# A decoder-layer step: the recurrence's levels two steps apart, the first transfers in another order, and half of the third chunk's post norm in that chunk's later stream

## The chip, the cores and the metric

The kernel runs on one core of one Trainium2 chip. Its time is the device time of one launch in microseconds (us). Each of the core's engines works through its own list of instructions in order: PE (TensorE) multiplies matrices, DVE (VectorE) and ACT (ScalarE) do the elementwise work, POOL (GpSimd) some of it, and SP (SyncE) mostly issues transfers between the chip's main memory and the core's on-chip memory. An instruction that waits holds up what stands behind it on its engine.

## The reference, cut to what matters

One layer of a decoder, in fp32, for 1,024 prompt tokens and for 8 running sequences with 8 new tokens each:

```
x = x + 1/2 * post1(swiglu_1(pre1(x)))                       # first feed-forward, D_FF = 2816
z = pre_mix(x) @ w_in + b_in                                  # q, k, v, f, i, gates in one projection
a = window attention, window 128, 8 heads, learned sinks      # sample: over cached keys and values
h = HGRN2 gated linear recurrence, 4 heads of 128 x 128       # sample: from a cached state
x = x + post_mix(concat(norm(a), gate(h)) @ w_out)
x = x + 1/2 * post2(swiglu_2(pre2(x)))                        # second feed-forward
```

The `pre` and `post` functions are RMS norms with a gain. The recurrence within a block of 128 tokens is computed by doubling: a level h = 1, 2, 4, ..., 64 joins neighbouring stretches of h tokens, multiplies queries and keys by the decays of those stretches, and yields the part of the attention-like matrix in which a query reads a key of the stretch before.

## The kernel before, in words

**Chunks.** The 1,088 tokens go in three chunks: chunk 0 has 320 columns (256 prompt tokens and the 64 of the samples) and is kept with features on the partitions; chunks 1 and 2 have 384 prompt tokens each. Every fp32 product is made of three products on split operands (`mm3`, lines 245, 246 and 247). The split is made on the core: a transfer brings a raw tile, ACT casts its high part (line 222), DVE subtracts to get the low part (line 223). Weights come into a ring of three raw tiles and leave as `wsph`/`wspl` (or `w`) tiles, of which there are eight.

**The feed-forward's second half** for chunks 1 and 2 is done by seven products of half-size operands. `pair(ms)` (from line 999 on) runs the products named in `ms` in turn: `PA` = (1, 6, 2) before the mixing, `PB` = (5, 3) behind chunk 0's input projection, then (7,) and (4,). For each group of two row blocks it needs a weight tile (line 951 or 954) and an activation tile `ar` (line 966), which is read back from main memory, cast by ACT and subtracted by DVE. Behind chunk 0's projection only one such `ar` tile is fetched ahead. The product's results are gathered from the PSUM banks by DVE (line 979) and, for product 5, by ACT as well (line 989); product 7 adds on POOL too (line 995). There are four `mm` banks; a group holds three.

**Side work.** What is not a feed-forward or projection product is written as generators that stop at each `yield`. `tick()`, called between groups of matmuls, advances them: named streams by a fixed rate, and two queues, `at` (attention) and `hg` (recurrence), at the pace at which the steps counted for a chunk end by its due tick (132, 208 and 256). The number beside a generator in a queue is the count of its steps. `intra(n)` (line 1250 on) is the recurrence inside the blocks of chunk n: for each level the matmuls `lv` (line 1267, up to h = 16) or `l` (line 1307, h = 32 and 64), the copies into `cm` (line 1297) or by ACT, and the multiplications of the queries by the decays on DVE (line 1316) and of the keys on POOL (line 1318). It stops once after each level.

**Post norm of chunks 1 and 2.** `half_n(y, hf, ...)` squares half of a chunk's columns on ACT (line 384), fetches a gain row (`gb`, line 377) and multiplies on DVE (line 388), three steps. `half1(n)` starts that for one half as the stream `half`, and `done1(n)` starts the stream `c1` or `c2` with the other half, then `post_n` (which reads x, writes `x1N` and normalises) and `pre_n` (the transposes `tr`, with ACT line 432 and DVE line 433 forming the projection's operand).

**The head.** `pre_first` forms chunk 0's first operands and issues, on SP, the loads of the first weight tiles (line 229) and of the rows of x (line 635), whose squares ACT sums (line 642) for the first norm. `wts.fill(k)` issues weight loads until k are ahead.

The written order is not the last word: within the dependences a scheduling pass settles each engine's list, so a moved step can move others.

Of the kernel before, what the change touches and what calls it, by code (L numbers as in the profile page):

```python
# [27 lines left out]
NPB = [2, 3, 3]  # L28
# [16 lines left out]
def tile_step(ctx: ExitStack, tc: tile.TileContext, A: dict, O: dict):  # L45
# [50 lines left out]
    def stream(name, gen, rate):  # L96
        streams[name] = [gen, rate, 0.0]
# [447 lines left out]
    def pre_first(wgu, h, wts):  # L545
# [83 lines left out]
        sm = small()  # L629
        V.memset(sm[:, 0], 1.0)  # L630
        rows = []
        for i in range(3):
            r = rows_of(0, i)
            t = big(F32, (P, D))
            nc.sync.dma_start(t[:r], A["x_prompt"][0, i * P:(i + 1) * P] if i < 2 else
                              A["x_sample"].rearrange("b t d -> (b t) d"))
            rows.append(t)

        def squares(i):
            r = rows_of(0, i)  # L640
            t = rows[i][:r]
            do("ACT", lambda: S.activation(t, t, AF.Square, scale=RMS, accum_out=sm[:r, 0, i:i + 1]))

        squares(0)
        squares(1)
        with queued("ACT"), queued("DVE"):
            wts.fill(2)
        last["ACT"], last["DVE"] = formed[1].ins, formed[0].ins
        squares(2)
        do("ACT", lambda: S.activation(junk[:, :P], ones, AF.Silu))  # L650
        do("DVE", lambda: V.tensor_scalar(ms0[:, 0:3], sm[:, 0, 0:3], EPS, None, op0=ALU.add))
        root(sm[:, 1, 0:3], ms0[:, 0:3])
# [390 lines left out]
    def mixing(tp, h):  # L1043
# [206 lines left out]
        def intra(n):  # L1250
# [40 lines left out]
            while h <= 64:  # L1291
# [37 lines left out]
                            G.tensor_copy(Av[:, j, :, r], C[r, j])  # L1329
                h *= 2  # L1330
                yield
            z["K"], z["D"] = K, Ds[0]

        def finish_hgrn(n, bank, r, c0):
# [182 lines left out]
        def ready(kind, n):  # L1517
            if n not in MT:
                MT[n] = new_h(n)
            if kind == "at":  # L1520
                gens = [(attn_block(n, b), 9) for b in range(NPB[n])]
                if n == 0:
                    gens += [(sample_attn(), 11), (kv_out(0), 1)]
                if n == 2:
                    gens.append((kv_out(2), 1))
            else:
                gens = [(intra(n), 8)] + [(hgrn_block(n, b), 3) for b in range(NPB[n])]
                if n == 0:
                    gens.append((sample_hgrn(), 14))
                if n == 2:  # L1530
                    gens.append((state_out(), 1))
            queues[kind] += [[n, g, left] for g, left in gens]
# [77 lines left out]
    def done1(n):  # L1610
        y, g = f1.ys[n], cols[:, C_MPRE:C_MPRE + 8]
        if n == 0:
            stream("c0", seq(post_t(y, A["x0T"], halfpost[:, 0:8], x1T, ms0), pre_t(y, g, hmix)), RA0)
        else:
            need("half")
            stream(f"c{n}", seq(half_n(y, 2 - n, sums[n], A["norm_ffn1_post"]),
                                post_n(n, y, sums[n], xN[n - 1], x1N[n - 1]), pre_n(n, y, g, hmix)), RA1)

    def half1(n):
# [38 lines left out]
    with tc.tile_pool(name="mx", bufs=1) as tp:  # L1658
        w_in_units, w_out_units = mixing(tp, hmix)
        need("c0")  # L1660
        now[0] = 0
        w_in_units(0)
        half1(1)
        f1.pair(PB, False, last=lambda: f1.begin_pair((7,), False))
        done1(1)
        f1.pair((7,), False, last=lambda: f1.begin_pair((4,), False))
        half1(2)
        f1.pair((4,), False)
        done1(2)
        need("c1")  # L1670
        w_in_units(1)
        need_mix(0)
        w_out_units(0, ym, sums)
        done_mix(0)
        need("c2")
        w_in_units(2)
        need("c0")
        f2.head(range(HEAD2[0]))
        need_mix(1)
        w_out_units(1, ym, sums)  # L1680
        done_mix(1)
        f2.head(range(HEAD2[0], HEAD2[1]))
        need("c1")
        need_mix(2)
        w_out_units(2, ym, sums)
        done_mix(2)
# [128 lines left out]
```

## Time and profile before

| | us |
|---|---|
| median of three runs | 1952.87 |
| the three runs | 1950.09, 1952.87, 1953.01 |
| the profiled execution | 1954.31 |
| its span (first to last instruction) | 1952.6 |
| PE busy in it | 1937.5 (99%) |
| DVE, ACT, POOL busy | 1349.6 (69%), 929.0 (48%), 211.1 (11%) |
| mean granted TensorE clock | 0.998 |

A row of a timeline gives start, busy time, engine, source line, operation, result and operands; in brackets stands the idle time of the engine before it and what ended it. The records of back-to-back matmuls overlap, so the time that one costs is read from one start to the next: 0.23 us for a 512-column one, 0.15 us for a 320-column one. The chain of waits follows the program's end back, piece by piece, to what released each piece.

### The profile page before, as it was taken

What the parts mean: (1) busy time and instruction counts of PE and PEld (TensorE: products, weight loads), DVE (VectorE), ACT (ScalarE), POOL (GpSimd) and SP (SyncE); (2) the same over time, 40 slices, a digit from 0 to 9 for tenths busy, and PEclk for the clock granted to TensorE, in tenths of its full rate; (3) what the DMA queues carried; (4) which work ended last, traced back from release to release, by engine and by line L of the source; (5) the groups of instructions that cost most, each with busy time, mean ns of one, the idle gap of its engine ahead of it and who ended that gap; (6) DMA issues with size and microseconds to landing.
All of it is one profiled execution on the core that took longest, in us unless ns stands there. A gap on an engine that the chain in (4) does not pass through costs nothing.

```text
span 1952.6 us, 34158 instructions
## 1 busy us (share of the span) xinstructions
PE 1937.5 (99%) x13451; PEld 1825.4 (93%) x13451; DVE 1349.6 (69%) x2188; ACT 929.0 (48%) x1637; POOL 211.1 (11%) x213
## 2 busy tenths in 40 slices
PE   9999999999999999999999999999999999999998
PEld 9999999999998987788899898999999999999887
DVE  5876667776558666875667765745987877655666
ACT  6633333444445544654345455745544444444453
POOL 0000000000004112111232431101000000000202
PEclk9999999999999999999999999999999999999999
DMA  9643345556677555675434333556555645577974
GB/s 322 209 143 129 144 162 186 179 183 208 236 236 228 163 146 163 213 228 153 120 101 141 115 112 117 190 166 206 174 204 187 217 177 186 206 237 232 308 260 141
DMA packets 162492, 362.65 MB, mean 186 GB/s; under 512 B 16524, under 2 KB 60236, under 8 KB 162316
## 3 DMA queue, kind: packets, MB, share of 16 engines
q1 hardware_dynamic: 161324, 358.65, 55.5%
q8 instruction: 105, 1.72, 0.4%
q10 hardware_dynamic: 1008, 1.84, 0.3%
q14 instruction: 55, 0.45, 0.1%
HBM read 283.78 MB, written 77.63 MB: 185 GB/s over the span
## 4 chain that ended last, share of the span: by engine, by line
PE 94%; DMA 2%; DVE 2%; ACT 1%; issue 1%; POOL 0%; SPq 0%; DVEq 0%; POOLq 0%; ACTq 0%
PE mm L245 28%; PE mm L247 28%; PE mm L246 28%; PE c L247 1%; PE c L245 1%; PE c L246 1%; DMA ar<-fa 1%; PE pv L1234 1%; PE sc L1193 1%; PE pT L1219 1%; PE lv L1267 0%; DMA raw<-in_ffn_w_gu_dram 0%; DMA x1N<-big 0%; PE av L1368 0%; DMA big<-in_x0T_dram 0%
## 5 line engine op out<-in xcount | busy, mean ns | idle before, releaser
L245 PE MATMUL mm<-h,wsph 128*128 128x320 f32 (+1 forms) x1280 | 409.5, 320 | 0.2 <-DVE sg L702 0.2
L247 PE MATMUL mm<-h,wspl 128*128 128x320 f32 (+1 forms) x1280 | 403.5, 317 | 1.2 <-DVE wspl L223 1.2
L246 PE MATMUL mm<-h,wsph 128*128 128x320 f32 (+1 forms) x1280 | 404.4, 316 | 0.0
L223 DVE TENSOR_TENSOR wspl<-raw,wsph 128x1024 fp32r<-128x1024 f32 x200 | 250.0, 1251 | 156.4 <-ACT wsph L222 156.0
L222 ACT CAST wsph<-raw 128x1024 fp32r<-128x1024 f32 x200 | 209.3, 1048 | 270.6 <-PE mm L246 205.4
L222 ACT CAST w<-raw 128x512 fp32r<-128x512 f32 (+1 forms) x226 | 169.3, 754 | 240.3 <-PE mm L246 119.8
L223 DVE TENSOR_TENSOR w<-raw,w 128x512 fp32r<-128x512 f32 (+1 forms) x226 | 196.6, 874 | 87.8 <-ACT w L222 87.3
L245 PEld LDWEIGHTS mm<-h,wsph 128*128 128x128 f32 x1280 | 240.4, 188 | 5.4 <-issue 3.2
L247 PEld LDWEIGHTS mm<-h,wspl 128*128 128x128 f32 x1280 | 239.9, 188 | 3.0 <-DVE wspl L223 1.7
L246 PEld LDWEIGHTS mm<-h,wsph 128*128 128x128 f32 x1280 | 240.5, 188 | 1.5 <-issue 0.7
L245 PE MATMUL mm<-h,w 128*128 128x384 f32 x704 | 235.6, 335 | 0.0
L246 PE MATMUL mm<-h,w 128*128 128x384 f32 x704 | 235.6, 335 | 0.0
L247 PE MATMUL mm<-h,w 128*128 128x384 f32 x704 | 230.5, 335 | 0.0
L245 PE MATMUL mm<-w,h 128*128 128x512 f32 x462 | 182.2, 398 | 1.9 <-DVE big L979 1.0
L246 PE MATMUL mm<-w,h 128*128 128x512 f32 x462 | 181.0, 392 | 0.0
L247 PE MATMUL mm<-w,h 128*128 128x512 f32 x462 | 178.9, 392 | 0.0
L216 POOL TENSOR_TENSOR sm<-sm,mhalf 128x3 f32<-128x3 f32 (+4 forms) x37 | 33.7, 913 | 1187.6 <-DVE sm L304 462.3
L245 PEld LDWEIGHTS mm<-h,w 128*128 128x128 f32 x704 | 132.2, 188 | 0.2 <-ACT big L793 0.2
L222 ACT CAST w<-t 128x512 fp32r<-128x512 f32 x176 | 107.3, 621 | 52.4 <-PE mm L247 46.9
L246 PEld LDWEIGHTS mm<-h,w 128*128 128x128 f32 x704 | 132.1, 188 | 0.0
L247 PEld LDWEIGHTS mm<-h,w 128*128 128x128 f32 x704 | 131.7, 188 | 0.0
L223 DVE TENSOR_TENSOR w<-t,w 128x512 fp32r<-128x512 f32 x176 | 119.0, 687 | 10.5 <-ACT w L222 10.3
(348 smaller groups left out, 3688.5 us busy)
## 6 DMA issues: line engine op xcount, KB each, us to landing
raw<-in_ffn_w_gu_dram SPq DMA_DIRECT2D x154, 512.0 KB
raw<-in_ffn_w_down_dram SPq DMA_DIRECT2D x74, 512.0 KB
raw<-in_w_in_dram SPq DMA_DIRECT2D x54, 512.0 KB
ar<-fa SPq DMA_DIRECT2D x70, 384.0 KB
big<-in_ffn_w_down_dram SPq DMA_DIRECT2D x88, 256.0 KB
fb<-big SPq DMA_DIRECT2D x44, 512.0 KB
raw<-fb SPq DMA_DIRECT2D x40, 512.0 KB
fa<-big SPq DMA_DIRECT2D x22, 768.0 KB
```

The costliest lines, as they stand in the source:

```text
L216: G.tensor_tensor(y, x, mhalf[:y.shape[0], :y.shape[1]], op=ALU.pow)
L222: formed[1] = S.copy(hi, src)
L223: return (lo_eng or V).tensor_tensor(lo, src, hi.bitcast(F32), op=ALU.subtract)
L245: PE.matmul(out, a[0], b[0], start=first, stop=False, skip_group_check=resume)
L246: PE.matmul(out, a[0], b[1], start=False, stop=False, skip_group_check=resume)
L247: r = latest[0] = PE.matmul(out, a[1], b[0], start=False, stop=last, skip_group_check=resume)
L1193: PE.matmul(banks[g][:, i * 256:i * 256 + wk], zq[64 * g:64 * g + 64, 2 * pr + i, b * P:(b + 1) * P], kx[64 * g:64 * g + 64, k0:k0 + wk], ...
L1219: PE.transpose(bank[:, (i * nk + kb) * P:(i * nk + kb + 1) * P], pt[g][:, i, kb * P:(kb + 1) * P], ident)
L1234: PE.matmul(ob[q0:q0 + 64, c:c + 64], pT[g][:, k1:k1 + 64], vn[:, vb, g * 64:g * 64 + 64], start=kb == 0, stop=kb == nk - 1)
```

## The change: what it does

It has three parts.

1. In `pre_first`, the loads of the second and third block of rows of x, and the sum of squares of the second, are placed behind the issue of the second weight tile.
2. In `intra(n)`, a second `yield` follows each level but the last, so that each level takes two steps of its queue; the count of its steps goes from 8 to 14. (`h` has been doubled by then, so `h <= 64` holds for six of the seven levels.)
3. `half1(2)` is no longer called ahead of product 4; chunk 2's sums tile is only allotted there, and `done1(2)` runs both halves of the chunk in the stream `c2`, behind product 4.

```diff
@@ pre_first
-        for i in range(3):
+
+        def load_rows(i):
             r = rows_of(0, i)
             t = big(F32, (P, D))
             nc.sync.dma_start(t[:r], A["x_prompt"][0, i * P:(i + 1) * P] if i < 2 else
...
+        load_rows(0)
         squares(0)
-        squares(1)
         with queued("ACT"), queued("DVE"):
             wts.fill(2)
         last["ACT"], last["DVE"] = formed[1].ins, formed[0].ins
-        squares(2)
+        for i in (1, 2):
+            load_rows(i)
+            squares(i)
@@ intra
                 h *= 2
                 yield
+                if h <= 64:
+                    yield
@@ ready
-                gens = [(intra(n), 8)] + [(hgrn_block(n, b), 3) for b in range(NPB[n])]
+                gens = [(intra(n), 14)] + [(hgrn_block(n, b), 3) for b in range(NPB[n])]
@@ done1
-            stream(f"c{n}", seq(half_n(y, 2 - n, sums[n], A["norm_ffn1_post"]),
+            halves = (2 - n,) if n == 1 else (n - 1, 2 - n)
+            stream(f"c{n}", seq(*[half_n(y, hf, sums[n], A["norm_ffn1_post"]) for hf in halves],
                                 post_n(n, y, sums[n], xN[n - 1], x1N[n - 1]), pre_n(n, y, g, hmix)), RA1)
@@ step
-        half1(2)
+        sums[2] = small()
         f1.pair((4,), False)
```

The added lines shift the line numbers of the changed kernel by 1 to 3 inside `pre_first`, by 3 behind it and by 5 behind `intra`: its 966 is 969, its 979 is 982, its 1316 is 1319.

**The head, SP's list.** `raw` are weight tiles, `big` the rows of x. Before:

```order
L229 DMA raw_231<-in_ffn_w_gu_dram 128x1024
L635 DMA big_239<-in_x_prompt_dram 128x1024
L635 DMA big_241<-in_x_prompt_dram 128x1024
L635 DMA big_243<-in_x_sample_dram 64x1024
L229 DMA raw_247<-in_ffn_w_gu_dram 128x1024
```

Now:

```order
L229 DMA raw_231<-in_ffn_w_gu_dram 128x1024
L636 DMA big_239<-in_x_prompt_dram 128x1024
L229 DMA raw_242<-in_ffn_w_gu_dram 128x1024
L636 DMA big_248<-in_x_prompt_dram 128x1024
L636 DMA big_251<-in_x_sample_dram 64x1024
```

The second weight tile has moved ahead of two loads of x.

**The end of product 5, DVE's list.** `h<-ar` is the low part of an activation tile, `w<-raw` that of a weight tile, `cm<-lm,lv` and the row behind it a level of chunk 0's recurrence, and line 979 (982) the gathering of a bank. Before, from the third activation tile ahead of product 3 on:

```order
L223 TENSOR_TENSOR h_1047_7673<-ar_1048_7674,h_1047_7673 128x2x384
L1297 COPY_PREDICATED cm_948_6915<-lm8_87,lv_1005_7377 128x256
L1316 TENSOR_TENSOR big_898_6608<-big_898_6608,D_947_6914 128x4x16x8
L223 TENSOR_TENSOR w_1023_7527<-raw_1021_7524,w_1022_7526 128x1024
L223 TENSOR_TENSOR h_1049_7696<-ar_1050_7697,h_1049_7696 128x384
L979 TENSOR_TENSOR big_767_5843<-mm_977_7141,big_767_5843 128x512
```

Now:

```order
L223 TENSOR_TENSOR h_1044_7591<-ar_1045_7592,h_1044_7591 128x2x384
L223 TENSOR_TENSOR w_1021_7445<-raw_1019_7442,w_1020_7444 128x1024
L1162 TENSOR_TENSOR h_873_6452<-oT_1009_7361,h_871_6450 128x4x128
L1300 COPY_PREDICATED cm_948_6915<-lm4_88,lv_1010_7368 128x256
L1300 COPY_PREDICATED cm_948_6915<-lm4_88,lv_1010_7368 64x128
L1319 TENSOR_TENSOR big_898_6608<-big_898_6608,D_947_6914 128x4x40x4
L223 TENSOR_TENSOR h_1046_7614<-ar_1047_7615,h_1046_7614 128x384
L1407 COPY big_1161_8315<-kx_842_6247 128x8x8
L982 TENSOR_TENSOR big_767_5843<-mm_977_7153,big_767_5843 128x512
```

Level 8 stood behind the third activation tile; now level 4 stands there, with two more instructions ahead of it, and level 8 comes some twenty rows later.

**The same place, PE's list.** Product 5's last group is `mm_977` to `mm_979`; product 3 starts with `mm_1018` (before) and `mm_1016` (now). Before, from its first row on:

```order
L245 MATMUL mm_1018_7521<-w_1007_7415,h_1014_7448 128x512
L246 MATMUL mm_1018_7521<-w_1008_7416,h_1014_7448 128x512
L247 MATMUL mm_1018_7521<-w_1007_7415,h_1014_7448 128x512
L1267 MATMUL lv_1017_7475<-big_898_6608,K_946_6913 32x32 x32
L245 MATMUL mm_1018_7521<-w_1007_7415,h_1014_7448 128x512
L246 MATMUL mm_1018_7521<-w_1008_7416,h_1014_7448 128x512
L247 MATMUL mm_1018_7521<-w_1007_7415,h_1014_7448 128x512
L245 MATMUL mm_1019_7522<-w_1007_7415,h_1014_7448 128x512
```

Now, from the last three rows of `mm_1016` ahead of the level:

```order
L245 MATMUL mm_1016_7439<-w_1012_7415,h_1022_7448 128x512
L246 MATMUL mm_1016_7439<-w_1013_7416,h_1022_7448 128x512
L247 MATMUL mm_1016_7439<-w_1012_7415,h_1022_7448 128x512
L1196 MATMUL sc_1031_7502<-kx_842_6247,big_853_6314 128x256
L1196 MATMUL sc_1032_7503<-kx_842_6247,big_853_6314 128x256
L1270 MATMUL lv_1035_7520<-big_898_6608,K_946_6913 32x32 x4
L245 MATMUL mm_1017_7440<-w_1005_7334,h_1014_7419 128x512
```

Twelve rows of `mm_1016` and four of `sc` now stand between product 5's last row and the level's first matmuls, where three rows of `mm_1018` stood.

**Product 4, ACT's list and SP's.** `h<-ar` on ACT is the high part of product 4's first activation tile, line 384 the squares of `half_n`. ACT before:

```order
L432 ACTIVATE h_1114_8054<-tr_1129_8103,cols_78 128x384
L384 ACTIVATE junk_73,sm_1120_8070<-big_976_7140 128x512 x2
L222 CAST h_1127_8080<-ar_1128_8081 128x2x384
L222 CAST w_1147_8198<-raw_1146_8196 128x1024
L432 ACTIVATE h_1114_8054<-tr_1130_8109,cols_78 128x384
```

Now:

```order
L432 ACTIVATE h_1113_8054<-tr_1118_8064,cols_78 128x384
L1167 ACTIVATE junk_73,sm_1129_8105<-t2_1128_8103 128x512
L222 CAST h_1126_8080<-ar_1127_8081 128x2x384
L222 CAST w_1146_8203<-raw_1145_8201 128x1024
L432 ACTIVATE h_1113_8054<-tr_1131_8117,cols_78 128x384
```

SP before:

```order
L377 DMA gb_1131_8118<-in_norm_ffn1_post_dram 128x512
L954 DMA raw_1146_8196<-fb1_102 128x2x512
L954 DMA raw_1154_8271<-fb1_102 128x512
L966 DMA ar_1128_8081<-fa1_101 128x2x384
L229 DMA raw_1166_8354<-in_w_in_dram 128x1024
```

Now:

```order
L957 DMA raw_1145_8201<-fb1_102 128x2x512
L957 DMA raw_1152_8245<-fb1_102 128x512
L1403 DMA vnew_1159_8311<-vsc_8309 8x4x128
L1403 DMA vnew_1160_8312<-vsc_8309 8x4x128
L377 DMA gb_1170_8352<-in_norm_ffn1_post_dram 128x512
L969 DMA ar_1127_8081<-fa1_101 128x2x384
```

The squares no longer stand ahead of the cast; on SP two small loads of the sample attention (`vnew`) and the gain row of the half now stand between the last weight tile and the activation tile.

## The prediction

> **What bounds the kernel now.** I read the page's busy times and its chain of waits first, then the list of what PE waits for, then windows over the places where PE is not full.
>
> ```profile
> PE 1937.5 (99%) x13451; PEld 1825.4 (93%) x13451; DVE 1349.6 (69%) x2188; ACT 929.0 (48%) x1637; POOL 211.1 (11%) x213
> PE 94%; DMA 2%; DVE 2%; ACT 1%; issue 1%; POOL 0%; SPq 0%; DVEq 0%; POOLq 0%; ACTq 0%
> ```
>
> PE is the bound: it is busy for 99% of the span, and the chain that ends last lies on it for 94%. The change takes no matmul away, so it can only give back time in which PE stands still or runs slowly. That stock is small:
>
> ```profile
> PE lv L1267 <- DVE big L1316: 2.1, 1, 2.1
> PE mm L247 <- DVE wspl L223: 1.2, 2, 0.7
> PE mm L561 <- DVE sm L630: 1.1, 1, 1.1
> PE mm L245 <- DVE big L979: 1.0, 1, 1.0
> PE tr L428 <- DVE h L433: 0.9, 1, 0.9
> PE mm L245 <- ACT h L222: 0.9, 1, 0.9
> PE pv L1234 <- DVE t L1222: 0.8, 1, 0.8
> ...
> 0.00:25.00 25.00, 23.21 (x150) 22.57 (x151) 13.44 (x34) 15.37 (x26) 2.03 (x10) 1.00 0.93 318
> 750.00:775.00 25.00, 21.95 (x187) 17.00 (x188) 18.72 (x31) 12.48 (x21) 6.42 (x11) 0.86 0.63 187
> 800.00:825.00 25.00, 23.15 (x129) 18.20 (x128) 19.38 (x37) 15.06 (x32) 7.22 (x5) 1.00 0.44 142
> 825.00:850.00 25.00, 25.00 (x156) 22.10 (x155) 19.80 (x34) 14.61 (x30) 2.28 (x3) 1.00 0.53 162
> ```
>
> In the windows the second number is PE's busy time, and the last three are clock, DMA share and GB/s. PE's waits add up to 8.0 us here. To them comes a stretch at a granted clock of 0.86, 0.14 x 25 = 3.5 us. So some 11 us of 1952.6 are to be had at all. A difference of 0.2%, about what a measurement of this kernel can tell from no change, is 3.9 us. The change must win a third of everything to be seen.
>
> **Part 1, the head.** The second weight tile comes late, and PE waits for its low part:
>
> ```profile
> 6.08 2.25 SPq L635 DMA_DIRECT2D big<-in_x_prompt_dram  x2
> 8.99 8.67 DMA raw<-in_ffn_w_gu_dram
> 17.68 1.06 ACT wsph L222
> 18.76 1.24 DVE wspl L223
> 20.04 0.41 PE L247 MATMUL mm<-h,wspl 128*128 128x320 f32 x1 [0.66 <-DVE wspl L223]
> 22.37 1.22 DVE L223 TENSOR_TENSOR wspl<-raw,wsph 128x1024 fp32r<-128x1024 f32 x1 [0.60 <-ACT wsph L222]
> 24.19 0.31 PE L247 MATMUL ax<-h,wspl 128*128 128x320 f32 x1
> ```
>
> Now one x load (1.1 us of issuing, half of the 2.25) and the sample's are no longer ahead of it, nor their 512 + 256 KB (128 and 64 rows of 1,024), which at the 318 GB/s of that window are 2.4 us. It lands about 2.4 us earlier, and its cast precedes the square of the second x block. The 0.66 us go entirely, and with the pipeline's refill up to 0.8 us. But the third tile does not come earlier: its cast stands on ACT behind the squares, which wait for the x blocks that are now later, and its low part, which waited 0.60 for that cast, ends at 23.59. PE would ask for it 0.8 us before 24.19, at 23.4, and waits 0.2 again; and in ACT's new list a gate (`sg`, line 702) is put ahead of the fourth cast. So I take **-0.4 us**, between -0.8 and 0.
>
> **Part 2, the levels, at the end of product 5.** This is the costliest place:
>
> ```profile
> 729.05 2.35 DVE L223 TENSOR_TENSOR h<-ar,h 128x768 fp32r<-128x768 f32 x1
> 731.42 3.35 DMA ar<-fa
> 731.32 0.61 DVE L1297 COPY_PREDICATED cm<-lm,lv 128x256 f32<-128x256 uint8 x2
> 731.84 0.81 DVE L1316 TENSOR_TENSOR big<-big,D 128x640 f32<-128x640 f32 x1
> 744.00 5.05 DMA ar<-fa
> 749.99 0.96 DVE L223 TENSOR_TENSOR h<-ar,h 128x768 fp32r<-128x768 f32 x1 [4.80 <-ACT h L222]
> 750.98 2.48 DMA ar<-fa
> 751.19 0.69 DVE L1316 TENSOR_TENSOR big<-big,D 128x512 f32<-128x512 f32 x1
> 752.03 0.75 PE L1267 MATMUL lv<-big,K 128*32 128x32 f32 x64 [2.13 <-DVE big L1316]
> 755.31 0.80 PE L245 MATMUL mm<-w,h 128*128 128x512 f32 x1 [1.03 <-DVE big L979]
> 759.10 0.43 PE mm L247
> 769.36 1.06 PE sc L1193 x8
> ```
>
> PE waits for the recurrence's line 1316. But that multiplication itself was ready to run long before: it stood on DVE behind the low part of an activation tile (749.99), which had waited 4.80 us for a tile that landed at 749.05. These tiles come one after another: each is issued (the first, third and fourth of them at 731.42, 744.00 and 750.98) when the one before has been subtracted. The second wait, 1.03 us, is for a bank that line 979 frees behind the last such tile. So both waits hang on the chain of `ar` tiles; the level is only the first victim. In the chain the matmuls up to 759.10 take 0.43 us apiece, twice what the same ones take elsewhere (the 512-column rows' 0.23): the clock was halved for some 6.8 us, 3.4 us lost, which is the window's 3.5.
>
> Now level 8 is later, but level 4 has taken its place behind the third tile. How the new order comes out, by these rows: the first tile was held up by a low part of 2.35 us, where the others take 0.96. If that is a collision with something beside it, it may or may not recur: the chain comes 0 to 1.4 us earlier, and I take 0.7, the middle. The third tile's low part then ends at 750.95 - 0.7 = 750.3. Behind it DVE has a weight's low part (1.2, as at 22.37), a line-1162 step (0.6, taken as large as the copies), two copies (0.61 together) and the level on 640 columns (0.81): 753.5. PE is at the level after nine more 512-column matmuls (2.0) and four `sc` (0.5), less 32 `lv` (0.75) than before, so at 751.6, and waits 1.9 us. Then come the last tile's low part (0.56 for half the size, by the others' 0.96), a small copy and line 982 (as 1316, 0.69): 754.9, where PE waits 1.3 us for the bank. It starts 0.4 us earlier than 755.31, and by the two lists has done six 512-column matmuls (1.4) and the `sc` (0.5) more and 60 `lv` (1.4) less, 0.5 us more work. **-0.9 us**, between +0.1 (the chain not earlier, the `lv` dearer) and -1.6. The waits, 3.2 us together, stay what they were, so I leave the clock's loss at 3.4 us.
>
> The Trainium skill (TensorE: Matmul & The Clock Gate, Part 1: The HAM clock gate) describes a clock that is halved after an idle window of about 3.4 us, counted in windows that run freely; and its section "Why this matters for your kernels" allows PE gaps of up to some 3 us. Here the halving followed an idle time of 2.13 us, so the trace is stricter than that allowance; the length, two windows, agrees. By the allowance alone the new waits would cost no clock, and the sum would be 3.4 us lower; that is the first rival below.
>
> In chunks 1 and 2 the levels move by tens of rows and the attention with them. There the windows are full, but for one place:
>
> ```profile
> 1138.60 1.15 PE L1234 MATMUL pv<-vn,t 128*64 128x64 f32 x32 [0.75 <-DVE t L1222]
> ```
>
> In the new list this `pv` meets other neighbours (up to -1.0), and one later `pv` stands only some 0.7 us of PE work behind the copy that it reads, which costs 0.3 to 1. I take **0**, between -1 and +1. The extra steps themselves issue nothing: a `yield` is no instruction.
>
> **Part 3, half of chunk 2's norm.** It moves three squares (ACT, 0.63 each), three multiplications (DVE, 0.69 each, as line 1316's of that size) and a gain row's transfer out of product 4:
>
> ```profile
> 806.68 7.48 SPq L954 DMA_DIRECT2D raw<-fb  x2
> 814.25 0.39 SPq L966 DMA_DIRECT2D ar<-fa  x1
> 814.93 2.27 POOL big L995
> 816.64 0.55 PE L428 MATMUL tr<-ident,big 128*128 128x128 f32 x3 [0.95 <-DVE h L433]
> 817.22 0.63 ACT L384 ACTIVATE junk<-big 128x512 bf16<-128x512 f32 x1 [1.33 <-POOL big L995]
> 818.72 0.50 PE L245 MATMUL mm<-w,h 128*128 128x512 f32 x1 [0.90 <-ACT h L222]
> ```
>
> Product 4's first matmul waits for the cast of its `ar` tile, and the cast stood behind the square, which waited for POOL. That goes: with the square away the cast runs when the tile lands, 814.25 + 2.5 to 3.4 = 816.8 to 817.6 by the two shorter `ar` transfers, 0.2 to 1.1 us earlier. Against that, SP's list now has two `vnew` and the gain row ahead of the tile, three issues of 0.4 each: 1.2 us later. The first wait (0.95) is for line 433 on DVE, while POOL's adds run, and they stay. Between them PE has other rows than before. I take **-0.4 us** of the 1.85, between -1.85 and +1.2. The moved half, 2.1 us of DVE and 1.9 of ACT, falls on 825 to 850, where DVE has 5.2 us to spare and ACT 10.4; chunk 2's projection waits for its stream only after all of chunk 1's. Uncovered it would cost those 2.1 us.
>
> **Sum.** -0.4 - 0.9 + 0 - 0.4 = -1.7 us against the profiled execution, 1954.31: 1952.6. That execution lies 1.4 us above the median of the runs, 1952.87, so for a run I say **1951.2 us**.
>
> **The rivals.**
>
> (a) *The clock is not halved.* Whether it is seems to be a matter of how much idle time falls in one stretch. Now it would be 1.9 and 1.3 us with matmuls between instead of 2.13 at once. If that is enough, or the chain of `ar` tiles comes the full 1.4 us earlier, 3.4 us more are won: 1947.8; with the other lower bounds 1944. For it: two waits of 0.9 us within 2 us at 816 to 819 did not halve the clock (1.00 in that window). Against it: the two waits together are as long as before.
>
> (b) *It grows at product 4 and the time is longer.* The mechanism is SP's list: `ar` now stands behind three more issues, each of which can also wait for its own buffer. If the tile lands 1.2 us later and nothing is won from ACT, PE's idle time before product 4's first matmul is 0.9 + 1.2 = 2.1 us, which at 752 was enough to halve the clock: +1.2 + 3.4 = +4.6 at this place, with -0.4 at the head and nothing at product 5: 1957.1. The point from which it decides is an idle time of some 2.1 us. For it: no issue on SP is free, and the last weight's issue there already waited until 814.16. Against it: the square's 0.63 and its wait for POOL (1.33) no longer stand before the cast.
>
> (c) *Nothing moves.* The levels were not what was late, so the waits pass to the bank and to the next reader of the same chain, the head gives its gain back at the third tile: 1952.9, give or take 1.
>
> **How the numbers follow.** The forecast gets 0.35, (a) 0.32, (b) 0.20, (c) 0.13. Faster by over 0.2% (below 1949.0): nearly all of (a), a fifth of the forecast: 0.38. Slower (above 1956.8): most of (b) and a little of the rest, 0.19. The same: 0.43. The range is 1944 to 1957.5: from (a) with the other gains to (b). The forecast's own is 1949 to 1954.
>
> **What would show it.** In the changed kernel's trace: the wait before the PE row at 20 us gone, and a small one before the `ax` row at 24; near 752 a wait of `lv` for line 1319 of some 1.9 us and then of `mm` for line 982 of 1.3, with the `ar` tiles still one after another, and matmuls at 0.43 us after it (their absence is (a)); near 818 a wait of product 4's first matmul for the cast of its tile, whose issue follows `vnew` and `gb`, of 1 to 1.6 us (2.1 and a clock below 1.00 is (b)). I am wrong if `lv` waits for nothing there, if the tiles come much earlier or later than 0.7 us, or if over 2 us are won or lost in the recurrences of chunks 1 and 2.

## The result

The changed kernel takes 1962.34 us, the median of six runs (1957.99 to 1965.28), against 1950.53 us of the kernel before, six runs on the same chip (1949.95 to 1953.01). The ratio is 1.0054, with a 95% interval of 1.0043 to 1.0064. The change makes the kernel slower by half a per cent, some 10.5 us. I had said 1951.2 us, and at most 1957.5.

Its profiled execution took 1961.9 us (span 1960.2), 7.6 us more than the one of before. That one (1954.31) was one of the longer executions of its kernel: later runs of before lie between 1948.6 and 1957.8 us, with medians of 1951 to 1953. Four later executions that were longer by hundreds of us or more (two of before, at 4907 and 4923 us, one of e2 at 2370 and one of e5 at 2658) are left out of every ratio.

From the page of the changed kernel, the busy times and the chain of waits by engine:

```profile
PE 1940.8 (99%) x13451; PEld 1827.4 (93%) x13451; DVE 1347.3 (69%) x2188; ACT 927.0 (47%) x1636; POOL 207.8 (11%) x213
PE 88%; DMA 5%; DVE 3%; ACT 1%; issue 1%; SPq 0%; POOL 0%; DVEq 0%; POOLq 0%; ACTq 0%
```

The matmuls are the same, but PE is busy for 3.3 us more and stands idle for 4.3 us more, and more of the chain lies on transfers (5% for 2%). What PE waits for most in the changed kernel (total, times, longest):

```profile
PE pv L1237 <- DVE t L1225: 4.5, 2, 2.4
PE mm L245 <- ACT h L222: 1.9, 1, 1.9
PE sav L1498 <- DMA big<-in_state_hgrn_dram: 1.5, 1, 1.5
PE tr L428 <- DVE big L1506: 1.1, 1, 1.1
```

And its windows (PE's busy time second; clock, DMA share and GB/s last):

```profile
750.00:775.00 25.00, 24.56 (x235) 19.35 (x233) 14.63 (x27) 12.40 (x22) 4.71 (x4) 1.00 0.63 196
775.00:800.00 25.00, 23.28 (x169) 18.92 (x170) 19.62 (x38) 15.73 (x39) 5.75 (x10) 0.93 0.73 239
1275.00:1300.00 25.00, 24.77 (x211) 23.36 (x212) 14.84 (x31) 15.65 (x27) 0.56 (x1) 0.93 0.42 132
```

The wait of `lv` is gone, and with it the slow clock of the window from 750 us on (1.00 for 0.86). But a wait that was not there before heads the list, `pv` for the copy of the transposed probabilities (line 1225), and two windows have a clock of 0.93 (0.07 x 25 = 1.75 us lost in each). The first such place, in rows of the chain and of the engines' timelines:

```profile
729.04 0.95 DVE L223 TENSOR_TENSOR h<-ar,h 128x768 fp32r<-128x768 f32 x1
735.91 3.33 DMA ar<-fa
741.17 3.28 DMA ar<-fa
751.15 1.27 DVE L982 TENSOR_TENSOR big<-mm,big 128x512 f32<-128x512 f32 x2
758.96 1.22 ACT t L1213 x6
767.67 6.49 DMA ar<-fa
775.10 0.96 DVE L223 TENSOR_TENSOR h<-ar,h 128x768 fp32r<-128x768 f32 x1 [1.47 <-ACT h L222]
775.98 0.68 DVE L1225 COPY t<-pT 128x512 f32<-128x512 f32 x1
776.72 1.24 PE L1237 MATMUL pv<-vn,t 128*64 128x64 f32 x32 [2.16 <-DVE t L1225]
780.18 0.63 PE L247 MATMUL mm<-w,h 128*128 128x512 f32 x1
```

At the end of product 5 the chain of activation tiles came 4.6 us earlier than before (the third landed at 741.17 + 3.28 = 744.45 for 749.05), line 982 ran at 751.15, and nothing waited. The same chain then broke down one product later: the softmax (line 1213) of chunk 0's second block now stands among product 3's tiles, the next tile is issued at 767.67 and lands at 774.16, and the copy that `pv` needs stands on DVE behind that tile's low part. The second place:

```profile
1272.15 0.72 PE L1222 MATMUL pT<-ident,t 128*128 128x128 f32 x4
1272.29 1.98 ACT L222 CAST wsph<-raw 128x1024 fp32r<-128x1024 f32 x2
1273.35 1.23 DVE L223 TENSOR_TENSOR wspl<-raw,wsph 128x1024 fp32r<-128x1024 f32 x1 [2.57 <-ACT wsph L222]
1274.50 0.68 DVE L1225 COPY t<-pT 128x512 f32<-128x512 f32 x1
1275.23 0.45 PE L1237 MATMUL pv<-vn,t 128*64 128x64 f32 x8 [2.36 <-DVE t L1225]
```

Here `pv` stands on PE directly behind the transposes `pT`, with no other work between. The copy waits on DVE behind a weight's low part, which waits for two casts on ACT. And in the sample's recurrence:

```profile
885.96 0.55 PE L428 MATMUL tr<-ident,big 128*128 128x128 f32 x3 [1.14 <-DVE big L1506]
886.42 3.76 SPq L1465 DMA_DIRECT2D t<-osc  x9
890.22 0.40 SPq L1484 DMA_DIRECT2D big<-in_state_hgrn_dram  x1
894.62 1.07 PE L1498 MATMUL sav<-big,t 128*32 128x128 f32 x16 [1.52 <-DMA big<-in_state_hgrn_dram]
```

The state's transfer is issued behind nine small ones of the sample's attention, and PE waits for it. The two waits before product 4, which the prediction's third part speaks of, stand in PE's timeline so:

```profile
813.38 1.07 PE L428 MATMUL tr<-ident,big 128*128 128x128 f32 x6 [0.34 <-DVE h L433]
816.35 0.50 PE L245 MATMUL mm<-w,h 128*128 128x512 f32 x1 [1.90 <-ACT h L222]
```

The tile of that cast, in the chain of waits:

```profile
810.01 5.43 DMA ar<-fa
```

It is issued at 810.01, earlier than before (814.25), but its transfer takes 5.43 us, where the prediction reckoned with 2.5 to 3.4.

### The profile page after: what moved, and what is told of

The parts are those of the page before. It is cut to its first block, busy times and chain, and to the rows that moved or that the text cites. A ratio compares the mean times of both kernels' runs of the same rounds, so it can differ in the third digit from the quotient of the medians.

```text
span 1960.2 us, 34134 instructions
## 1 busy us (share of the span) xinstructions
PE 1940.8 (99%) x13451; PEld 1827.4 (93%) x13451; DVE 1347.3 (69%) x2188; ACT 927.0 (47%) x1636; POOL 207.8 (11%) x213
## 4 chain that ended last, share of the span: by engine, by line
PE 88%; DMA 5%; DVE 3%; ACT 1%; issue 1%; SPq 0%; POOL 0%; DVEq 0%; POOLq 0%; ACTq 0%
PE mm L245 27%; PE mm L247 26%; PE mm L246 26%; DMA ar<-fa 1%; PE c L245 1%; PE c L247 1%; PE c L246 1%; DMA xt<-in_x_prompt_dram 1%; DMA raw<-in_ffn_w_gu_dram 1%; PE pv L1237 1%; PE sc L1196 1%; DVE wspl L223 1%; PE lv L1270 1%; PE pT L1222 1%; DMA big<-in_x_sample_dram 0%
```

## The experiments

The theories: **A**, the levels' two steps lose, by moving the attention so that `pv` stands too close behind `pT`; **B**, the moved half of the post norm loses; **C**, the added steps lose in another way, and other waits would take the place of these; **D**, the waits at 750 to 780 us hang on the chain of activation tiles. E and F came later. The diffs are against the kernel before unless "whole change" stands there.

### The parts alone (e1 to e4)

e1, only the levels:

```diff
                 h *= 2
                 yield
+                if h <= 64:
+                    yield
...
-                gens = [(intra(n), 8)] + ...
+                gens = [(intra(n), 14)] + ...
```

> Only the levels two steps apart, nothing else of the change. Theory A: this part carries the loss. Its lists on PE have the same two short distances between the transposes pT and the pv that reads their copy as the changed kernel (about 2.8 us of PE work at 774 us, none at 1272 us), so it shows the same waits of pv for the copy, 2.2 and 2.4 us with slow matmuls behind them, and no wait of lv near 752. Time 8 to 12 us above before, like the whole change. Rival B: the half of the post norm is what loses (the later stream of chunk 2 holds up the transfers near 885 us): then this kernel lacks the waits near 885 to 893, and is at most 5 us above before.

Measured: 1962.04 us, ratio 1.0041 (1.0028 to 1.0054). Its profile has the wait that heads the changed kernel's list:

```profile
PE pv L1234 <- DVE t L1222: 5.1, 2, 2.7
```

Two things differ from the whole change. The waits at 885 to 895 us are not in it, though the kernel is as slow. And in the window from 900 us on PE never stands idle, yet the clock reads 0.93:

```profile
900.00:925.00 25.00, 25.00 (x138) 22.08 (x137) 12.25 (x17) 9.54 (x10) 1.90 (x1) 0.93 0.60 168
```

Right ahead of the slow stretch stand two state updates `su` (897.96 and 899.38) with one matmul between them; e16 below comes back to these.

e2, only the half:

```diff
-        half1(2)
+        sums[2] = small()
...
+            halves = (2 - n,) if n == 1 else (n - 1, 2 - n)
```

> Only the half of chunk 2's post norm moved into that chunk's later stream. Theory A: within 2 us of before; the wait of lv near 752 and the halved clock behind it stay (some 7 us), the waits at 815 to 819 change by at most 1 us. Rival B: 4 to 6 us above before, with waits of PE near 885 to 893 for the sample's recurrence and its state's transfer.

Measured: 1953.51 us, ratio 1.0003 (0.9994 to 1.0011).

e3, only the head (the diff of `pre_first`):

> Only the head's transfers reordered. Both theories: 0.5 us less than before, from the wait at 20 us, which loses its 0.7; nothing else moves, since the lists behind the head are the same but for names. A difference of over 1 us would show that an early shift of half a microsecond decides later waits.

Measured: 1951.52 us, ratio 0.9997 (0.9988 to 1.0006).

e4, the head and the half, without the levels:

> The change without its levels. Theory A: the loss is gone: within 2 us of before, with the wait of lv near 752 back. Rival B: still 4 to 6 us above before.

Measured: 1951.87 us, ratio 0.9997 (0.9988 to 1.0005).

So the levels alone carry the loss, and B falls. Two expectations of these four failed in part. In e3 "nothing else moves" did not hold: its profile has new waits of 0.25, 0.28 and 0.71 us for weight tiles, at 23 to 29 us, and no wait of `lv`. In e2, too, the wait of `lv` at 752 and the slow clock were gone, though its list is that of before at this place. That matters for reading the profile of before. e2's profile shows only the wait for the bank:

```profile
753.34 0.51 PE L245 MATMUL mm<-w,h 128*128 128x512 f32 x1 [1.41 <-DVE big L979]
```

The profiles of e3, e5, e14 and e16 show the same 1.41 us there and no wait of `lv`. e4's has the wait of `lv` (2.0 us) again, 1.7 us for the bank and a clock of 0.93. So this 6.7 us of the profile of before (2.13 + 1.03 of waiting and 3.5 of clock) falls in some executions and not in others: of seven profiles with the list of before at this place, two have the stop.

### The levels by chunk (e5, e6)

```diff
-                if h <= 64:
+                if h <= 64 and n > 0:        # e5; e6: n == 0
```

> The levels two steps apart in chunks 1 and 2 only; chunk 0 as before. Theory A (what loses is the short distance on PE between pT and the pv that reads its copy): in this kernel's list the shortest of these distances is 1.9 us of PE work where the changed kernel has none, so no wait of pv of over 1 us, the wait of lv near 752 as before, and a time within 3 us of before. Rival C (the levels' own extra steps lose, by lateness of the recurrence in chunks 1 and 2): 4 us or more above before, with waits of PE for lines 1297, 1316 or 1318.

Measured: 1956.89 us, ratio 1.0022 (1.0013 to 1.0032). No wait of `pv` of over 0.3 us, but 4.4 us more than before, about where rival C's range begins; yet PE's longest new wait is 1.0 us, at 1129, and none is for the lines that C named. Behind that short wait the clock was halved (0.07 x 25 = 1.75 us):

```profile
1125.00:1150.00 25.00, 23.67 (x375) 22.04 (x362) 17.54 (x26) 15.23 (x25) 6.24 (x5) 0.93 0.31 99
```

And the score matmuls are dearer (columns: count, then busy time and mean of one), here and in the profile of before:

```profile
L1193 PE MATMUL sc<-kx,big 64*128 64x256 f32 (+1 forms) x120 | 18.8, 395 | 0.0
```

```profile
L1193 PE MATMUL sc<-kx,big 64*128 64x256 f32 (+1 forms) x120 | 16.6, 395 | 0.0
```

Two half blocks have their eight records parted into four and four, with other matmuls between, and each four takes as long (1.13 us) as eight together elsewhere:

```profile
1050.40 1.13 PE L1193 MATMUL sc<-kx,big 64*128 64x256 f32 x4
1052.72 1.13 PE L1193 MATMUL sc<-kx,big 64*128 64x256 f32 x4
```

> The levels two steps apart in chunk 0 only; chunks 1 and 2 as before. Theory A: no wait of lv near 752 (3 to 7 us won), the wait of pv near 774 as in the whole change (4 us lost), and two places later, near 1215 to 1240 us, where pv stands right behind pT (none and 0.15 us of PE work between): a wait of 2 to 2.5 us at each. Time 3 to 6 us above before. Rival C: within 2 us of before, since chunks 1 and 2 have their old steps.

Measured: 1967.17 us, ratio 1.0074 (1.0061 to 1.0087), the dearest of all. The two places where `pv` stands right behind `pT` have become one long stop:

```profile
1252.16 0.45 PE L1234 MATMUL pv<-vn,t 128*64 128x64 f32 x8 [2.26 <-DVE t L1222]
1253.85 1.40 PE L1234 MATMUL pv<-vn,t 128*64 128x64 f32 x24 [1.24 <-ACT t L1222]
```

The waits came where A said, but the sum was three times too small. Part of what it left out is the clock, 0.93 in three windows (775, 900 and 1250 us); in the one at 900, as in e1, PE never stands idle. Chunks 1 and 2 had their old steps here, and yet their attention had moved: the two queues are stepped together, so six more recurrence steps in chunk 0 also take attention steps earlier (44 attention steps by the end of chunk 0's time, for 40 before, counted in the program), and what follows is paced anew.

### Taking the short distances away (e7, e9, e10)

e7, the levels and one more step between `pT` and `pv` everywhere:

```diff
                     pT.append(t)
                 yield
+                yield
                 if ob is None:
...
-                gens = [(attn_block(n, b), 9) for b in range(NPB[n])]
+                gens = [(attn_block(n, b), 11) for b in range(NPB[n])]
```

> The levels two steps apart, and one more step between pT and pv in the attention's generator (its count 9 becomes 11). Theory A: the shortest distances are 1.1 and 1.7 us of PE work instead of none, so the waits of pv shrink from 5.1 us together to under 2.5; time 4 us or more below the levels alone, within 3 us of before. Rival C: the waits of pv go, but the time stays 8 us or more above before, since other waits take their place.

Measured: 1959.69 us, ratio 1.0034 (1.0022 to 1.0047). `pv` waits for 0.9 us, as A said, but the time is 7 us above before, not within 3: a transpose of the output now stands too close behind its norm.

```profile
1153.14 0.63 PE L1172 MATMUL oT<-ident,t 128*128 128x128 f32 x4 [2.59 <-DVE t L1167]
```

e9, the whole change, with that step only for the two half blocks that had waited:

```diff
                 yield
+                if (n, b, pr) in ((0, 1, 0), (2, 2, 0)):
+                    yield
                 if ob is None:
```

> The whole change, with one more step between pT and pv in just two of the sixteen half blocks of the attention: the ones whose pv waits at 774 and at 1272 us. In its list all sixteen distances from pT to pv are 2.5 us of PE work or more. Theory A: the waits of pv for the copy (4.5 us together, with 3 us of slow matmuls behind them) go, and the time falls by 5 to 8 us from the whole change's, to within 4 us of before. Rival C: other waits take their place and it stays 8 us or more above before.

Measured: 1962.65 us, ratio 1.0063 (1.0049 to 1.0077): no gain at all, as C said. No `pv` waits, and behind 821 us PE waits for nothing of note up to 1300. PE stands idle for 4.1 us less than in the changed kernel (15.3 for 19.4), but is busy for 4.6 us more (1945.4 for 1940.8). Two things took the place, in PE's timeline and in the groups of matmuls (count, busy time, mean of one; the last row is that of before):

```profile
781.65 0.53 PE L245 MATMUL mm<-w,h 128*128 128x512 f32 x1 [3.21 <-DVE big L982]
```

```profile
L1196 PE MATMUL sc<-kx,big 64*128 64x256 f32 (+1 forms) x120 | 18.8, 395 | 0.0
L1506 PE MATMUL su<-t,m 32*128 32x512 f32 x16 | 7.9, 640 | 0.0
```

```profile
L1499 PE MATMUL su<-t,m 32*128 32x512 f32 x16 | 4.5, 640 | 0.0
```

The stop at 774 came back at 778 with another victim, and the score matmuls and the state updates `su` take 18.8 and 7.9 us, where before they take 16.6 and 4.5: 5.6 us in which PE is busy, and which no list of waits shows. A further wait of 1.71 us stands at 818, and the clock reads 0.93 in two windows (775 and 800 us).

e10, the added step, but the queue's count left at 8:

> The levels two steps apart, but the count left at 8, so that the queue's pace is not raised for them. In its list one pv stands 0.15 us of PE work behind pT (near 1120 us), the others 2.2 or more. Theory A: one wait of pv of 2 to 2.5 us, 3 to 6 us above before. Rival (it is the raised pace as such): no such wait, within 2 us of before.

Measured: 1961.75 us, ratio 1.0055 (1.0042 to 1.0068). The time is as much above before as the whole change's, but the `pv` that the list put 0.15 us behind `pT` did not wait. PE's longest wait is another, and the clock was not halved behind it (1.00 in every window):

```profile
1289.77 0.41 PE L245 MATMUL mm<-h,wsph 128*128 128x320 f32 x1 [3.17 <-ACT sg L696]
```

So theory A in its narrow form falls. Take its victim away, and the time stays, or comes back elsewhere. The raised pace is not needed for the loss either.

### The chain of activation tiles (e8, e11, e12, e13, e15)

e8, the kernel before with two tiles ahead:

```diff
-            AC[ms] = Ahead([... for m in ms for ks in GROUPS], 2 if inner else 1)
+            AC[ms] = Ahead([... for m in ms for ks in GROUPS], 2)
```

> The kernel before, with two activation tiles fetched ahead in products 5, 3, 7 and 4 instead of one. Theory D (the wait near 752 hangs on the chain of these tiles, each issued when the one before is subtracted): lv no longer waits near 752 and the clock is not halved there: 3 to 7 us below before. Rival (the level itself is late): the wait stays at 2 us and the time within 1 us of before.

Measured: 1949.12 us, ratio 0.9981 (0.9972 to 0.9990), faster than both kernels. `lv` did not wait, and of the waits at 815 to 819 (1.85 us) 0.2 was left. Since `lv` did not wait in e2 and e5 either, one profile does not show that the second tile removed it; that all eleven runs lie within 1947.3 to 1950.5, where before spreads from 1948.6 to 1955.2, fits it.

> The head's order and the moved half, the levels as before, and two activation tiles ahead in products 5, 3, 7 and 4. If the gains are independent: the 3.7 us that two tiles ahead gave, and 0.5 of the head: 3 to 5 us below before. If the moved half needs what the second tile takes (buffers, transfers), no better than two tiles ahead alone.

Measured: 1949.28 us, ratio 0.9986 (0.9977 to 0.9994): 2.5 us below before, nothing beyond e8. The expected 3 to 5 us were not reached.

e12, the whole change with two tiles ahead, and e13, e9 with two tiles ahead:

> The whole change, with two activation tiles ahead in products 5, 3, 7 and 4. Theory D (the wait at 774 us is that of a copy of pT on DVE standing behind the chain of activation tiles): that wait of 2.2 us and the halved clock behind it go, 3 to 5 us below the whole change, so 5 to 8 us above before; the wait of pv at 1272 us stays. Rival (pv's place alone decides): the wait at 774 stays at 2 us, the time as the whole change.

> The whole change, with one more step before the two pv and two activation tiles ahead. Theory D: the wait of 3.2 us for line 982 at 778 goes too, no wait of over 2 us is left, and the time is 4 to 7 us below the two pv alone (1962.65), that is 1956 to 1959. What is left above before is then no wait of PE but dearer matmuls (those of sc and su took 5.2 us more there). Rival: the wait stays or comes back elsewhere, and the time stays above 1960.

Measured: e12 1963.35 us, ratio 1.0051 (1.0037 to 1.0065); `pv` waits longer at 774 us, 3.4 us. e13 1958.24 us, ratio 1.0028 (1.0018 to 1.0039): the waits behind 813 us went, but line 982 is still waited for, for 3.0 us at 780. So the depth of one tile is not what makes this stop, and e13's time lies in D's range without D's reason. One clause of its expectation held: PE stands idle for 13.5 us in e13, less than the 15.1 of before, so what e13 still loses is time in which PE is busy.

e15, the whole change, with the attention of chunk 0's second block put back by as many steps as it had been pulled forward:

```diff
             ob = None
+            for _ in range(4 if (n, b) == (0, 1) else 0):
+                yield
```

> The whole change, with four empty steps ahead of the attention of chunk 0's second block, as many as the added recurrence steps had pulled it forward. Theory F (the softmax that has moved between product 3's activation tiles holds up their chain, since its steps stand ahead of the casts on DVE and ACT): the wait of 2 to 3 us at 774 to 780 us goes, and the halved clock with it: 3 to 6 us below the whole change. Rival: the wait at that place stays, whichever instruction has it, and so does the time.

Measured: 1958.67 us, ratio 1.0038 (1.0025 to 1.0050), 3.7 us below the whole change's median in another series (3.1 by the ratios, whose intervals overlap). No wait is left between 757 and 806 us, and the clock there is 1.00, so theory F holds for that place. Part of the gain went again, to product 4, where the clock reads 0.86 in the window from 800 us on:

```profile
814.37 0.80 PE L245 MATMUL mm<-w,h 128*128 128x512 f32 x1 [3.12 <-ACT h L222]
```

### Matmuls that run beside each other (e14, e16)

The state updates, in the profile of before and then in that of the changed kernel:

```profile
863.80 1.13 PE L1499 MATMUL su<-t,m 32*128 32x512 f32 x4
```

```profile
899.77 1.12 PE L1504 MATMUL su<-t,m 32*128 32x512 f32 x2
905.71 1.12 PE L1504 MATMUL su<-t,m 32*128 32x512 f32 x2
```

A head's two updates use different quarters of the array's rows. Next to each other, all four records take 1.13 us; with other matmuls between them, two records take that long. Theory E says that the new list parts such partners, as e5's list does with its score matmuls.

e14 changes the order of a half block's four score matmuls, which stay together:

```diff
-                for i in range(2):
-                    for g in range(2):
+                for g in range(2):
+                    for i in range(2):
                         PE.matmul(banks[g][:, i * 256:i * 256 + wk],
```

> The kernel before, with only the order of the four score matmuls sc of each half block changed: the two that use the same half of the array follow each other, instead of taking turns. The same matmuls, operands and banks. Theory E (two matmuls on different halves of the array run side by side only when they stand next to each other): of the four pairs of records of a half block one stays, so its 1.06 us become 1.7 to 1.9, and the sum over sixteen 10 to 13 us more than before. Rival (the order does not matter on PE): within 1 us of before.

Measured: 1950.61 us, ratio 0.9989 (0.9980 to 0.9997), and the scores' group is as before:

```profile
L1193 PE MATMUL sc<-kx,big 64*128 64x256 f32 (+1 forms) x120 | 16.7, 396 | 0.0
```

So E in its first form falls: the order inside a closed group does not matter. (That the time is a little below before has no cause that I can name.) e16 parts the two updates of each head by other matmuls:

```diff
-                yield
                 for hf in range(2):
+                    if hf:
+                        yield
                     ub = axbank("su").rearrange("p (b t) -> p b t", b=4)
```

> The kernel before, with a step's end put between the two state updates su of a head of the sample's recurrence instead of ahead of both: in its list the four pairs are parted by 19 to 69 rows, all else stands as before. Theory E in its new form (partners on different parts of the array run side by side only with no other matmul between them): each pair takes 1.05 us more, 4.2 us in all. Rival (it costs nothing on the path): within 1 us of before.

Measured: 1958.09 us, ratio 1.0037 (1.0023 to 1.0050):

```profile
L1500 PE MATMUL su<-t,m 32*128 32x512 f32 x16 | 9.0, 640 | 0.0
```

The updates take 9.0 us for 4.5, so each parted pair costs 1.1 us, as expected. The kernel loses some 7 us in all. In the profiled execution another 1.75 us is a clock of 0.93 in the window from 800 us on, ahead of the parted updates; whether the edit brought it is not shown. The four parted pairs alone, without any wait, cost more (4.5 us) than the stop at 774 or the one at 1272 us (3.9 and 4.1 us).

## Why the prediction was wrong

**What bounds the kernel** was right as far as it went: PE, with about 11 us to be had. The error was in reading this as the whole account. It says what the change could win; what it could lose has no such bound.

**The base.** I took the profile as 1.4 us above the median and otherwise typical; by the six runs of the result it lies 3.8 us above. Its largest item, the 6.7 us at 752, is not in most executions: with the same list there, five of seven profiles have 1.41 us. What the change could win at this place was in most executions about a fifth of what I read from it.

**Part 1, the head**, -0.4: the wait of 0.66 us at 20 us is gone in every profile with the new head, and in this one nothing stands in its place. In four others (e3, e11, e12, e13) weight tiles are waited for at 23 to 29 us, for 0.3 to 1.2 us together, where the prediction had named a small wait; at its largest that is more than the gain. e3 alone, 0.9997, does not tell the part from nothing. The mechanism was right; that it came to -0.7 here, with no wait behind it, was luck of this execution.

**Part 2, the end of product 5**, -0.9: the order of steps was right (weight, line 1162, two copies, level 4, tile, small copy, line 982), and the step that failed is "I take 0.7" for how much earlier the chain of tiles comes. It came 4.6 us earlier: the low part of 2.35 us took 0.95, and the second and third transfers took 3.3 us each where they had taken over 5 (744.00 in the prediction's rows, and the one ahead of it):

```profile
736.70 5.36 DMA ar<-fa
```

So all 6.7 us went, as rival (a) had it and more. Only a part of this lead is the change's. From the start of the first low part to that of the third it is 20.9 us in before and 20.8 in e4, 18.0 to 18.5 in the five profiles with the same list and no stop, and 16.3 to 16.4 with the new levels in chunk 0 (the changed kernel, e1, e6, e9, e15). So some 2 us come with the change, 1.4 of them from the first low part (2.35 us in all seven, 0.95 in these); the other 2.5 are slow transfers of the execution that I started from.

**"I take 0" for the recurrences and the attention elsewhere** is the step that made the prediction wrong. What stands against the 6.7, from the rows above: at 774 us 2.16 of waiting and 1.75 of clock, which I had not looked at; at 885 to 895 us 1.14 + 1.52, likewise; at 1272 us 2.36 and 1.75. The last is the `pv` that I had found in the list "some 0.7 us of PE work behind the copy" and priced at 0.3 to 1. The price was wrong because I counted the copy's own time and not what stands ahead of it: on DVE a weight's low part, on ACT two casts. And dearer matmuls: `su` 5.6 us for 4.5, one parted pair. These places together cost 3.9 + 2.7 + 4.1 + 1.1 = 11.8 us, where the prediction had 0, between -1 and +1; for chunk 0's attention and the sample's recurrence it had no term at all.

**Part 3**, -0.4: product 4 waits 0.34 and 1.90 us, for 1.85 before, so +0.4, inside the bounds. The issue of the tile did fall behind `vnew` and `gb`, as rival (b) had it, but it came earlier than before; what was late was the landing, after 5.43 us. No clock was lost there. e2 and e4 show that the part costs nothing that can be measured.

Together: -0.7 - 6.7 + 3.9 + 2.7 + 4.1 + 1.1 + 0.4 = +4.8 us of the 7.6 between the two profiles. The other 2.8 us are in many pieces of a few tenths, and I can't name them. The gap between the medians is larger because the base had the stop. Against e2's profile, which has none (PE busy for 1936.8 us of a span of 1949.4), the changed kernel's PE is busy for 4.0 us more and idle for 6.8 more. The same pieces, with -1.41 us at product 5 and 0.34 + 1.90 - 0.89 = +1.4 us at product 4, come to -0.7 - 1.4 + 11.8 + 1.4 = 11.1 us, for these 10.8. So in this pair the listed places account for the loss; it is one pair of executions.

**The rivals.** (a)'s outcome came at its own place and was outweighed; it came by a lead of the chain far beyond the 1.4 us that (a) allowed, and most executions of before do not have the stop either, so this was in part luck. (b) gave the right sign with the wrong mechanism: the idle time of some 2.1 us from which it was to decide is not such a point (the last section). No rival said that steps which "issue nothing" move all the side work, through queues that are stepped together and a scheduling pass, to places that no one had chosen. All three signs in "what would show it" came: `lv` waits for nothing there, the tiles came much earlier than 0.7 us, and over 2 us were lost where the levels of chunks 1 and 2 had moved the attention (at 1272 us); but as much was lost in chunk 0's attention, at 774, which no sign named.

**What is settled, and what is not.** The levels alone carry the loss (e1 against e2 to e4). That added steps shift the attention and the sample's work is seen in the lists, and at one place putting the attention back took the stop away (e15). But no single stop is the cause: each repair (e7, e9, e12, e13, e15) left 5 to 12 us, with other victims. That the list of before is better suited as a whole is what remains. Why it is, I have not shown.

## What to carry to other kernels

In this kernel, whose main engine is 99% busy, the places that the side work had were worth more than the stall that the change was to remove: a change of its pace, even by empty steps, puts every later piece of it anew, and each must be priced, with the queues ahead of its copy counted and not only the copy. Before a stall is taken as a gain, see whether other executions of the same list have it. And look at the busy time of small matmuls by group: partners that were parted cost time in which the engine is busy and nobody waits.

## What the runs showed of the hardware

Two matmuls on different parts of the array that follow each other start 6 to 7 ns apart in the trace's records of before (13 in e14's), and take together what one takes alone; with other matmuls between them each takes its own time, 1.1 us more for a pair of `su`. The Trainium skill (TensorE: Matmul & The Clock Gate, Part 3: Packing small matmuls — row/col tiling) describes the first, with starts about 4 ns apart; that a few other matmuls between the two undo it is seen here and not stated there.

The clock was halved behind idle times of 2.13 us (before), 2.16 and 2.36 us (after), and not behind one of 1.90 us; the Trainium skill (TensorE: Matmul & The Clock Gate, Why this matters for your kernels) puts the gap to avoid at over some 3 us, so by these rows it is too high for this kernel. But the length of one wait does not decide it: the clock was halved behind 1.04 us in e5 and, in e1, behind no idle time at all, and it was not behind 3.17 us in e10 nor behind 2.35 us in e12, at the place of the 2.36. The windows that run freely, by the Trainium skill (TensorE: Matmul & The Clock Gate, Part 1: The HAM clock gate), would make the same idle time cost the clock in one execution and not in another. The traces agree: every half-clock stretch between the first and the last 10 us of a program is 3.41 or 6.83 us long, and between two of them lie whole multiples of 3.41 us. Cut along these windows, the place at 1272 us of the changed kernel and then of e12 reads (PE's busy time second, the clock third from the end):

```profile
1272.60:1276.01 3.41, 1.05 (x14) 0.73 (x15) 2.66 (x3) 3.39 (x4) 0.00 (x0) 1.00 0.15 14
1276.01:1279.42 3.41, 3.41 (x35) 2.56 (x32) 2.29 (x12) 0.47 (x2) 0.00 (x0) 0.50 0.75 247
```

```profile
1271.50:1274.91 3.41, 1.78 (x14) 1.39 (x12) 1.16 (x2) 3.41 (x9) 0.00 (x0) 1.00 0.00 0
1274.91:1278.32 3.41, 2.69 (x44) 2.18 (x45) 2.94 (x10) 1.96 (x3) 0.00 (x0) 1.00 0.63 166
```

PE is busy for 4.46 us in both pairs. In the first the idle time falls into one window and the next one has half the clock; in the second it is spread over two and none has. In the 18 profiles, away from the programs' ends, all 14 such windows in which PE was busy for at most 1.61 us are followed by half the clock. Of the fuller ones only six are: two that ran at half clock themselves (before, e15), one of 1.65 us (e4), one of 2.20 (e5), and in e1 and e6 a full one with parted `su`. So in these traces what a wait costs in clock hangs also on where it lies in these windows, which a list of instructions does not tell.
